# Gate and up by Strassen's seven products of 256 columns, second product in chunks of eight feature blocks

## The chip, the cores and the metric

The kernel runs on one core of one Trainium2 chip. The metric is the device time of one execution in microseconds. A core has five engines with instruction streams of their own: PE (TensorE, matrix products; its weight loads are listed apart as PEld), DVE (VectorE), ACT (ScalarE), POOL (GpSimd) and SP (SyncE, here only a queue that issues DMA transfers). Each engine works through its stream in order; semaphores join the streams.

## The reference, cut to what matters

512 tokens of width 1024 go through two layers. Per layer:

```
x <- x + 1/2 * SwiGLU_1(RMSNorm(x))
h  = RMSNorm(x);  P = h @ W_in          (gMLP, short convolution and retention mixers on P)
x <- x + concat(A, B, C) @ W_out
x <- x + 1/2 * SwiGLU_2(RMSNorm(x))
SwiGLU(x) = (silu(x @ w_gate) * (x @ w_up)) @ w_down        w_gate, w_up: 1024 x 2816, w_down: 2816 x 1024
```

A final RMSNorm follows. So there are four feed-forwards and two mixers, all in float32.

## The kernel before, in words

Activations lie with features on the 128 partitions and the 512 tokens along the free axis: x is eight tiles of 128x512 (`KT` = 8), the hidden layer 22 tiles (`FT` = 22, "feature blocks"). Every product is made of three matrix products: each operand is split into a high part in float32r (`xh`, `whi`, the left side of `h`) and the rest (`xl`, `wlo`), and `mm3` (L99 to L101) adds high*high, high*rest and rest*high into one PSUM bank. The split of an operand is a cast on ACT (L93 for weights, L113 for x) and a subtraction on DVE (L94, L114).

`gate_up` (L148) loops over the 22 feature blocks; for each it loads a gate and an up block of 128x1024 weights (512 KB each, `load`, four raw buffers, three pairs of split ones), does 24 matmuls of 512 columns for each, and `finish` scales by the token's 1/rms (`rr`), applies silu, multiplies and splits the result into `h`. When all 22 `h` exist, `ffn` (L216) runs the second product: eight output blocks `d`, each 66 matmuls of 512 columns, and after each the residual add and, in `after(d)`, the split of the new `x[d]` for the next stage and its square. 1/rms is made of those squares while the next stage's first blocks are multiplied: `norm_columns` (`pss`, L130) and `norm_rows` (`psr`, L144) each add a few small matmuls. `last_ffn` runs the last second product with tokens on partitions, in all eight PSUM banks. `start` (L187) lets the first products begin on half a weight block and the first x tile.

The order in which each engine issues is made by a scheduler when the program is built: it takes instructions by their place in the code and moves loads and splits ahead as far as buffers and its own estimate of times let it. Buffers are handed out by tag, a fixed number each.

Of the kernel before, what the change touches and what calls it, by code (L numbers as in the profile page):

```python
# [36 lines left out]
# Columns of the packed position constants.  # L37
# [5 lines left out]
def trunk(ctx, tc, xt, w_gu1, w_dn1, w_in, w_out, w_gu2, w_dn2, w_last, par, con, wst, bst, gain, out):  # L43
# [12 lines left out]
    def big(name, dt=F32):  # L56
        return hpool.tile([P, 2 * T], dt, tag="h", name=name)
# [20 lines left out]
    ct = cpool.tile([P, NCON], F32, name="ct")  # L78
# [3 lines left out]
    def weight_tiles():  # L82
        raw = wpool.tile([P, 1024], F32, tag="raw", name=uniq("raw"), bufs=4)
        hi = wpool.tile([P, 1024], F32R, tag="whi", name=uniq("whi"))
        lo = wpool.tile([P, 1024], F32R, tag="wlo", name=uniq("wlo"))
        return raw, hi, lo

    def load(src):
        """One block of weights as two float32r parts whose sum it is."""
        n = src.shape[-1]  # L90
        raw, hi, lo = weight_tiles()
        nc.sync.dma_start(raw[:, :n], src)
        nc.scalar.copy(hi[:, :n], raw[:, :n])  # L93
        nc.vector.tensor_tensor(lo[:, :n], raw[:, :n], hi.bitcast(F32)[:, :n], ALU.subtract)  # L94
        return hi, lo
# [7 lines left out]
    def split(h, lo, src):  # L103
        nc.scalar.copy(h, src)  # L104
        nc.vector.tensor_tensor(lo, src, h.bitcast(F32), ALU.subtract)  # L105
# [4 lines left out]
    def norm_part(k, gcol):  # L110
        """x[k] times its gain in two parts."""
        g = pcol[:, gcol + k : gcol + k + 1]
        nc.scalar.activation(xh[k], x[k], AF.Copy, scale=g)  # L113
        nc.vector.scalar_tensor_tensor(xl[k], x[k], g, xh[k].bitcast(F32), ALU.mult, ALU.subtract)  # L114

    def squares(k):
        if k == 0:
            state["acc"] = spool.tile([P, T], F32, tag="acc", name=uniq("acc"), bufs=1)
            nc.scalar.activation(state["acc"], x[k], AF.Square)
        else:  # L120
            sq = tpool.tile([P, T], F32, tag="sq", name=uniq("sq"))
            nc.scalar.activation(sq, x[k], AF.Square)
            nc.vector.tensor_tensor(state["acc"], state["acc"], sq, ALU.add)

    def norm_columns():
        """1 / rms of each token, as columns [token, chunk]."""
# [22 lines left out]
    def gate_up(l, w_gu, first=False):  # L149
        """h = silu(rms gate) * up, features on partitions."""  # L150
        hs = []
        waiting = []

        def finish(ps):
            rr = state["rr"]
            a = tpool.tile([P, T], F32, tag="a", name=uniq("a"))
            nc.vector.tensor_tensor(a, ps[0], rr, ALU.mult)  # L157
            nc.scalar.activation(a, a, AF.Silu)  # L158
            b = tpool.tile([P, T], F32, tag="b", name=uniq("b"))
            nc.vector.tensor_tensor(b, ps[1], a, ALU.mult)  # L160
            h = big(uniq("h"), F32R)
            split(h[:, :T], h[:, T:], b)
            hs.append(h)

        for f in range(FT):
            ps = []
            if first and f == 0:
                ps = start(w_gu[l, 0, 0], w_gu[l, 1, 0])
            else:
                for j in range(2):  # L170
                    hi, lo = load(w_gu[l, j, f])
                    p = bank(uniq("pgu"))
                    for k in range(KT):
                        c = slice(k * P, (k + 1) * P)
                        mm3(p, hi[:, c], lo[:, c], xh[k], xl[k], k == 0, k == KT - 1)
                    ps.append(p)
                    if f == 0 or first and f == 1:
                        (norm_columns, norm_rows)[j]()
            waiting.append(ps)
            if "rr" in state:  # L180
                while waiting:
                    finish(waiting.pop(0))
            yield hs

    def start(gate, up):
# [16 lines left out]
        for k in range(4, KT):
            nc.sync.dma_start(x[k], xt[:, k, :])
        for k in range(KT):
            norm_part(k, G1)
            for (raw, hi, lo), p in zip(w, ps):
                if k % 4 == 0:
                    c = half[k // 4]
# [4 lines left out]
        for k in range(KT):  # L213
            squares(k)
# [389 lines left out]
```

## Time and profile before

| | |
|---|---|
| median of 3 runs | 1877.07 us (1877.07 to 1877.4) |
| span of the profiled execution | 1875.7 us |
| PE, weight loads | 1865.6 us busy (99%), 1554.4 us (83%) |
| DVE, ACT, POOL | 839.3 us (45%), 567.2 us (30%), 27.4 us (1%) |
| DMA | 181.98 MB, 97 GB/s mean |

The profiled execution's own time is taken as its span, first to last instruction; the runs' median lies 1.4 us above it. Matmuls are pipelined, so a busy PE need not be at its peak: the spacing of matmul starts tells more than the busy share.

### The profile page before, as it was taken

To read this page: it belongs to the slowest core of one execution; us is meant where nothing else is said; L and a number is where in the kernel's file an instruction comes from. 1 tells how busy PE (TensorE), PEld (TensorE's weight loads), DVE (VectorE), ACT (ScalarE), POOL (GpSimd) and SP (SyncE) were. 2 spreads that over 40 slices of the span, in tenths; PEclk is the share of its full clock that TensorE was granted. 3 is DMA by queue.
4 is the path that set the end of the run, shared out by engine and by line. 5 is a ranking of instruction groups with operands and counts; after the bars stand their busy time and mean duration, and the time that the engine had idled before them with its cause. 6 is when DMAs were issued, how large, how long until landed. Compare 5 with 4: busy or idle time off the path is not lost.

```text
span 1875.7 us, 20497 instructions
## 1 busy us (share of the span) xinstructions
PE 1865.6 (99%) x8560; PEld 1554.4 (83%) x8560; DVE 839.3 (45%) x1052; ACT 567.2 (30%) x713; POOL 27.4 (1%) x34
## 2 busy tenths in 40 slices
PE   9999999999999999999999999999999999999998
PEld 7888888888888888888888888888888888888886
DVE  5344334474664434433443444344647543444224
ACT  5223222223343322322232232222132433323212
POOL 0000000000000000000000000000000000000000
PEclk9999999999999999999999999999999999999999
DMA  5232333322222232233323223333322222332321
GB/s 203 102 97 94 99 93 93 114 94 75 84 90 97 95 101 91 99 93 95 106 90 102 91 100 96 94 93 108 102 79 79 91 92 89 100 100 92 113 94 64
DMA packets 52860, 181.98 MB, mean 97 GB/s; under 512 B 6048, under 2 KB 6560, under 8 KB 52640
## 3 DMA queue, kind: packets, MB, share of 16 engines
q1 hardware_dynamic: 52624, 180.64, 29.8%
q8 instruction: 67, 1.10, 0.2%
q14 instruction: 25, 0.20, 0.0%
q10 hardware_dynamic: 144, 0.04, 0.0%
HBM read 178.56 MB, written 2.10 MB: 96 GB/s over the span
## 4 chain that ended last, share of the span: by engine, by line
PE 98%; issue 0%; ACT 0%; DMA 0%; DVE 0%; SPq 0%; POOL 0%; POOLq 0%; ACTq 0%
PE pgu L99 17%; PE pgu L100 17%; PE pgu L101 17%; PE pdn L101 8%; PE pdn L100 8%; PE pdn L99 8%; PE pqk L99 2%; PE pqk L101 2%; PE pout L100 2%; PE pout L99 2%; PE pqk L100 2%; PE pout L101 2%; PE pv L101 1%; PE pg L99 1%; PE pg L101 1%; PE pg L100 1%
## 5 line engine op out<-in xcount | busy, mean ns | idle before, releaser
L93 ACT CAST whi<-raw 128x1024 fp32r<-128x1024 f32 (+1 forms) x336 | 348.6, 1038 | 1184.7 <-issue 365.1
L99 PE MATMUL pgu<-xh,whi 128*128 128x512 f32 x1408 | 548.6, 390 | 1.2 <-ACT xh L113 1.2
L100 PE MATMUL pgu<-xl,whi 128*128 128x512 f32 x1408 | 548.0, 389 | 0.7 <-DVE xl L114 0.6
L94 DVE TENSOR_TENSOR wlo<-raw,whi 128x1024 fp32r<-128x1024 f32 (+1 forms) x336 | 405.1, 1206 | 319.3 <-ACT whi L93 305.2
L101 PE MATMUL pgu<-xh,wlo 128*128 128x512 f32 x1408 | 548.0, 389 | 0.0
L99 PEld LDWEIGHTS pgu<-xh,whi 128*128 128x128 f32 x1408 | 264.2, 188 | 56.4 <-ACT xh L113 1.7
L100 PEld LDWEIGHTS pgu<-xl,whi 128*128 128x128 f32 x1408 | 264.3, 188 | 55.8 <-DVE xl L114 1.5
L101 PEld LDWEIGHTS pgu<-xh,wlo 128*128 128x128 f32 x1408 | 264.3, 188 | 55.5 <-DVE wlo L210 0.3
L99 PE MATMUL pdn<-h,whi 128*128 128x512 f32 x528 | 205.4, 389 | 0.0
L100 PE MATMUL pdn<-h,whi 128*128 128x512 f32 x528 | 205.4, 389 | 0.0
L101 PE MATMUL pdn<-h,wlo 128*128 128x512 f32 x528 | 205.4, 389 | 0.0
L160 DVE TENSOR_TENSOR b<-pgu,a 128x512 f32<-128x512 f32 x88 | 60.8, 692 | 280.2 <-PE pgu L101 277.8
L157 DVE TENSOR_TENSOR a<-pgu,rr 128x512 f32<-128x512 f32 x88 | 60.8, 691 | 220.0 <-PE pgu L101 220.0
L100 PEld LDWEIGHTS pdn<-h,whi 128*128 128x128 f32 x528 | 99.1, 188 | 20.6
L101 PEld LDWEIGHTS pdn<-h,wlo 128*128 128x128 f32 x528 | 99.1, 188 | 20.6
L99 PEld LDWEIGHTS pdn<-h,whi 128*128 128x128 f32 x528 | 99.1, 188 | 20.5
L100 PE MATMUL pdn<-wlo,h 128*128 128x512 f32 x176 | 68.6, 390 | 0.0
L101 PE MATMUL pdn<-whi,h 128*128 128x512 f32 x176 | 68.5, 389 | 0.0
L99 PE MATMUL pdn<-whi,h 128*128 128x512 f32 x176 | 68.4, 389 | 0.0
L105 DVE TENSOR_TENSOR h<-b,h 128x512 fp32r<-128x512 f32 x88 | 60.2, 685 | 2.1 <-ACT h L104 2.1
L104 ACT CAST h<-b 128x512 fp32r<-128x512 f32 x88 | 54.7, 622 | 2.7 <-DVE b L160 2.5
L158 ACT ACTIVATE a<-a 128x512 f32<-128x512 f32 x88 | 55.0, 626 | 1.3 <-DVE a L157 1.3
(179 smaller groups left out, 1641.9 us busy)
## 6 DMA issues: line engine op xcount, KB each, us to landing
raw<-in_w_gu SPq DMA_DIRECT2D x174, 512.0 KB, 3.3
raw<-in_w_in SPq DMA_DIRECT2D x52, 512.0 KB, 3.3
raw<-in_w_dn SPq DMA_DIRECT2D x48, 448.0 KB, 3.3
raw<-in_w_dn SPq DMA_DIRECT2D x24, 512.0 KB, 3.5
raw<-in_w_last SPq DMA_DIRECT2D x22, 512.0 KB, 3.3
raw<-in_w_out SPq DMA_DIRECT2D x16, 512.0 KB, 3.3
x<-in_xt SPq DMA_DIRECT2D x8, 256.0 KB, 6.6
out<-o SPq DMA_DIRECT2D x8, 256.0 KB, 2.2
```

Of the source, the lines that this page charges most:

```text
L93: nc.scalar.copy(hi[:, :n], raw[:, :n])
L94: nc.vector.tensor_tensor(lo[:, :n], raw[:, :n], hi.bitcast(F32)[:, :n], ALU.subtract)
L99: nc.tensor.matmul(ps, lhsT=ah, rhs=bh, start=first, stop=False)
L100: nc.tensor.matmul(ps, lhsT=ah, rhs=bl, start=False, stop=False)
L101: nc.tensor.matmul(ps, lhsT=al, rhs=bh, start=False, stop=last)
L104: nc.scalar.copy(h, src)
L105: nc.vector.tensor_tensor(lo, src, h.bitcast(F32), ALU.subtract)
L157: nc.vector.tensor_tensor(a, ps[0], rr, ALU.mult)
L158: nc.scalar.activation(a, a, AF.Silu)
L160: nc.vector.tensor_tensor(b, ps[1], a, ALU.mult)
```

## The change

x, a 1024 x 512 matrix, and each pair of 1024 x 256 weight blocks are cut in halves along features and along tokens, so that a gate (or up) result of 256 features x 512 tokens is a 2 by 2 block product. Instead of its eight block products of 256 columns (24 matmuls each with the three parts, in the kernel before as 2 x 24 of 512 columns) it is made of seven (Strassen's, in Winograd's form): 7 x 4 pairs of x tiles x 3 parts = 84 matmuls of 256 columns. The unit is called a quad here; there are 22 per feed-forward (11 pairs of feature blocks, gate and up), 88 in all.

- x needs sums of its quarters: `norm_pair` makes, for each pair of x tiles, the forms S1, S2, S3, Z4 in float32 on DVE (128x256 each) and splits them; only ahead of a feed-forward (`sums`).
- The weights need sums: `load_quad` loads four quarters of 128x512 (columns A to D), loads the last one twice more, has a DMA from POOL add B and C to those copies, makes two more sums on DVE, and splits seven operands: `wd` and `wp` of 128x1024, `we`, `wf`, `wg` of 128x512.
- The results are put together from PSUM: products 1, 6, 7 and 4 add up in bank `pa`, 2 in `pb`, 5 and 3 in `pc`, and after each one ACT or DVE copies, adds or subtracts a quarter of 128x256 (L256 to L268). `WHEN` sets the order: product 1, 2 of a quad, 3 of the quad before, 6, 5, 4 of the quad before, 7. The tables `MOVING` and `WHEN` name them by number.
- The second product runs in three chunks of 8, 8 and 6 feature blocks after the gate and up of each, and adds to x three times; squares and norms follow the last chunk, once per pair of x tiles. Buffers: two raw weight tiles of 128x2560, three split tiles `w2`, five `w1`; work tiles come from pools opened per stage. `start` no longer starts on halves. In the mixer, the constants are loaded in each layer and the scores are made earlier.

```
-PIECES = ((0, 8), (8, 15), (15, 22))
+CHUNKS = ((0, 4), (4, 8), (8, 11))
+A11, A21, A12, A22, S1, S2, S3, Z4 = range(8)
...
+    def load_quad(src):
+        c = KP * P
+        raw = wpool.tile([P, 2560], F32, tag="raw", name=uniq("rawq"), bufs=2)
+        s = [raw[:, i * c : (i + 1) * c] for i in range(5)]
+        nc.sync.dma_start(raw[:, : 3 * c], src[:, : 3 * c])
+        two = raw[:, 3 * c :].rearrange("p (n c) -> p n c", n=2)
+        nc.sync.dma_start(two, src[:, 3 * c :].unsqueeze(1).broadcast_to([P, 2, c]))
+        nc.gpsimd.dma_start(raw[:, 3 * c :], src[:, c : 3 * c], accum_op=ALU.add)
+        d = wpool.tile([P, 2048], F32R, tag="w2", name=uniq("wd"), bufs=3)
+        parts(d[:, :1024], d[:, 1024:], raw[:, : 2 * c])
+        e = wpool.tile([P, 1024], F32R, tag="w1", name=uniq("we"), bufs=5)
+        parts(e[:, :c], e[:, c:], s[2])
+        nc.vector.tensor_tensor(s[2], s[2], s[3], ALU.add)
+        f = wpool.tile([P, 1024], F32R, tag="w1", name=uniq("wf"), bufs=5)
+        parts(f[:, :c], f[:, c:], s[2])
+        p = wpool.tile([P, 2048], F32R, tag="w2", name=uniq("wp"), bufs=3)
+        parts(p[:, :1024], p[:, 1024:], raw[:, 3 * c :])
+        nc.vector.tensor_tensor(s[0], s[0], s[2], ALU.add)
+        g = wpool.tile([P, 1024], F32R, tag="w1", name=uniq("wg"), bufs=5)
+        parts(g[:, :c], g[:, c:], s[0])
...
+    def norm_pair(m, gcol, sums):
+        xf[m] = xpool.tile([P, 16 * H], F32R, tag=f"xf{m}", name=uniq("xf"))
+        for k in (2 * m, 2 * m + 1):
+            g = pcol[:, gcol + k : gcol + k + 1]
+            nc.scalar.activation(xh(k), x[k], AF.Copy, scale=g)
+            nc.vector.scalar_tensor_tensor(xl(k), x[k], g, xh(k).bitcast(F32), ALU.mult, ALU.subtract)
+        if not sums:
+            return
+        v = spool.tile([P, 4 * T], F32, tag="xv", name=uniq("xv"), bufs=1)
+        for k in (0, 1):
+            g = pcol[:, gcol + 2 * m + k : gcol + 2 * m + k + 1]
+            nc.scalar.activation(v[:, k * T : (k + 1) * T], x[2 * m + k], AF.Copy, scale=g)
+        q = [v[:, i * H : (i + 1) * H] for i in range(8)]
+        nc.vector.tensor_tensor(q[S1], q[A21], q[A22], ALU.subtract)
+        nc.vector.tensor_tensor(q[S2], q[S1], q[A11], ALU.subtract)
+        nc.vector.tensor_tensor(q[S3], q[A11], q[A21], ALU.subtract)
+        nc.vector.tensor_tensor(q[Z4], q[S2], q[A12], ALU.add)
+        parts(xf[m][:, 4 * H : 8 * H], xf[m][:, 12 * H :], v[:, 2 * T :])
...
+    MOVING = {1: A11, 2: A12, 3: Z4, 4: A22, 5: S1, 6: S2, 7: S3}
+    WHEN = {1: 0, 2: 1, 6: 3, 5: 4, 7: 6, 3: 9, 4: 12}
+
+    def product(ps, n, w, first, pairs=range(KP)):
+        hi, lo = w[n]
+        for m in pairs:
+            bh, bl = form(m, MOVING[n])
+            c = slice(m * P, (m + 1) * P)
+            one = first and m == pairs[0]
+            nc.tensor.matmul(ps, lhsT=hi[:, c], rhs=bh, start=one, stop=False, skip_group_check=True)
+            nc.tensor.matmul(ps, lhsT=hi[:, c], rhs=bl, start=False, stop=False, skip_group_check=True)
+            nc.tensor.matmul(ps, lhsT=lo[:, c], rhs=bh, start=False, stop=m == pairs[-1], skip_group_check=True)
...
+            if n == 1:
+                nc.scalar.copy(c(A11), b["pa"])
+            elif n == 2:
+                nc.vector.tensor_tensor(c(A11), b["pb"], c(A11), ALU.add)
+            elif n == 6:
+                nc.scalar.copy(c(A12), b["pa"])
+            elif n == 5:
+                nc.scalar.copy(c(A22), b["pc"])
+            elif n == 7:
+                nc.vector.tensor_tensor(c(A22), c(A22), b["pa"], ALU.subtract)
+            elif n == 3:
+                nc.vector.tensor_tensor(c(A12), b["pc"], c(A12), ALU.subtract)
             else:
...
+                nc.scalar.copy(c(A21), b["pa"])
+                done(q)
...
+    def ffn(l, w_gu, w_dn, after):
+        with tc.tile_pool(name=uniq("ffn"), bufs=1, reuse_waits="tile") as pool:
+            stage["pool"] = pool
+            for i, (p0, p1) in enumerate(CHUNKS):
+                hs = gate_up(w_gu[l], p0, p1, i == 0)
+                down(l, w_dn, 2 * p0, hs, after if p1 == FP else lambda d: None)
```

`done` does what `finish` did, on 128x1024: for a gate quad the product with `rr` (L276, DVE) and silu (L277, ACT), for an up quad the product with the gate (L280, DVE) and the split into `h`.

DVE within gate and up. Before, the order repeats after two weight blocks (`wlo` a weight's rest, `a`, `b`, `h` the block's silu, product and split):

```order
L94 TENSOR_TENSOR wlo_794<-raw_792,whi_793 128x1024
L160 TENSOR_TENSOR b_756<-pgu_728,a_753 128x512
L94 TENSOR_TENSOR wlo_833<-raw_831,whi_832 128x1024
L105 TENSOR_TENSOR h_758<-b_756,h_758 128x512
L157 TENSOR_TENSOR a_823<-pgu_767,rr_323 128x512
L94 TENSOR_TENSOR wlo_864<-raw_862,whi_863 128x1024
```

In the change, one quad's share of the same stage; `g_`, `u_` are results of gate and up quads, `raw..885` the weights of the next quad but one to be multiplied:

```order
L88 TENSOR_TENSOR wd_889<-rawq_885,wd_889 128x1024
L88 TENSOR_TENSOR h_750<-u_528,h_750 128x1024
L258 TENSOR_TENSOR u_766<-pb_802,u_766 128x256
L88 TENSOR_TENSOR wp_899<-rawq_885,wp_899 128x1024
L266 TENSOR_TENSOR g_646<-pc_722,g_646 128x256
L88 TENSOR_TENSOR we_892<-rawq_885,we_892 128x512
L114 TENSOR_TENSOR rawq_885<-rawq_885 128x512
L119 TENSOR_TENSOR rawq_885<-rawq_885 128x512
L88 TENSOR_TENSOR wf_896<-rawq_885,wf_896 128x512
L276 TENSOR_TENSOR g_646<-g_646,rr_324 128x1024
L264 TENSOR_TENSOR u_766<-u_766,pa_788 128x256
L88 TENSOR_TENSOR wg_903<-rawq_885,wg_903 128x512
```

Two weight subtractions of 128x1024 per two blocks became two of 128x1024 and three of 128x512, two sums (L114, L119) and three steps from PSUM (L258, L266, L264) came in between, and `wp`, `L114` and what follows them wait for the adding DMA.

ACT in the same place. Before, a cast of weights alternates with a silu or a split of `h`:

```order
L93 CAST whi_622<-raw_621 128x1024
L104 CAST h_548<-b_546 128x512
L93 CAST whi_653<-raw_652 128x1024
L158 ACTIVATE a_613<-a_613 128x512
L93 CAST whi_692<-raw_691 128x1024
```

In the change, one quad's share; L256, L260, L262 and L268 are the copies out of PSUM:

```order
L87 CAST wg_785<-rawq_767 128x512
L87 CAST wd_889<-rawq_885 128x1024
L87 CAST h_750<-u_528 128x1024
L256 COPY u_766<-pa_788 128x256
L87 CAST wp_899<-rawq_885 128x1024
L87 CAST we_892<-rawq_885 128x512
L260 COPY u_766<-pa_788 128x256
L87 CAST wf_896<-rawq_885 128x512
L262 COPY u_766<-pc_842 128x256
L268 COPY g_646<-pa_668 128x256
```

The copy of product 1 (L256), which frees `pa` for product 6, now stands behind the casts of `wg` and `wd` and the split of `h` (or the silu).

DVE at the start of the program. Before, the splits of x (L114), the first half weights (L210) and the squares (L123) follow each other:

```order
L114 SCALAR_TENSOR_TENSOR xl_94<-x_78,pcol,xh_86 128x512
L114 SCALAR_TENSOR_TENSOR xl_95<-x_79,pcol,xh_87 128x512
L123 TENSOR_TENSOR acc_219<-acc_219,sq_224 128x512
L210 TENSOR_TENSOR wlo_132<-raw_130,whi_131 128x512
L210 TENSOR_TENSOR wlo_135<-raw_133,whi_134 128x512
L123 TENSOR_TENSOR acc_219<-acc_219,sq_227 128x512
L114 SCALAR_TENSOR_TENSOR xl_96<-x_80,pcol,xh_88 128x512
L114 SCALAR_TENSOR_TENSOR xl_97<-x_81,pcol,xh_89 128x512
```

In the change, 12 of the 48 DVE instructions that stand ahead of the first step out of PSUM; `xf` and `xv` are the forms of x and their sums for pair 0 (101), 1 (120, 125), 2 (139, 144) and 3 (158, 163):

```order
L88 TENSOR_TENSOR xf_139<-xv_144,xf_139 128x1024
L88 TENSOR_TENSOR wf_191<-rawq_180,wf_191 128x512
L119 TENSOR_TENSOR rawq_180<-rawq_180 128x512
L170 TENSOR_TENSOR xv_163<-xv_163 128x256
L168 TENSOR_TENSOR xv_163<-xv_163 128x256
L88 TENSOR_TENSOR wd_206<-rawq_202,wd_206 128x1024
L169 TENSOR_TENSOR xv_163<-xv_163 128x256
L88 TENSOR_TENSOR wg_198<-rawq_180,wg_198 128x512
L171 TENSOR_TENSOR xv_163<-xv_163 128x256
L88 TENSOR_TENSOR we_209<-rawq_202,we_209 128x512
L88 TENSOR_TENSOR wp_216<-rawq_202,wp_216 128x1024
L88 TENSOR_TENSOR xf_158<-xv_163,xf_158 128x1024
```

The splits of the first two quads' weights stand between the sums of the x pairs, and the split of pair 3's sums (`xf_158`) comes last.

## Rows read from the trace of the kernel before

**Rows 1.** The page: span, busy time by engine, granted clock by slice, chain by engine.
```profile
span 1875.7 us, 20497 instructions
...
PE 1865.6 (99%) x8560; PEld 1554.4 (83%) x8560; DVE 839.3 (45%) x1052; ACT 567.2 (30%) x713; POOL 27.4 (1%) x34
...
PEclk9999999999999999999999999999999999999999
...
PE 98%; issue 0%; ACT 0%; DMA 0%; DVE 0%; SPq 0%; POOL 0%; POOLq 0%; ACTq 0%
```

**Rows 2.** Chain that ended last, in order of time: start us, us, what.
```profile
25.76 0.79 PE pss L130 x8
...
375.80 0.79 PE pss L130 x8
...
581.64 0.79 PE pss L130 x8
...
942.57 0.79 PE pss L130 x8
...
1303.48 0.79 PE pss L130 x8
...
1860.47 0.76 DVE xtok L277
```

**Rows 3.** Timeline of PE in gate and up, 512 columns, first and last of 37 matmuls: start us, us, what.
```profile
17.21 0.39 PE L101 MATMUL pgu<-xh,wlo 128*128 128x512 f32 x1
...
25.37 0.39 PE L101 MATMUL pgu<-xh,wlo 128*128 128x512 f32 x1
```

**Rows 4.** Timeline of PE at the gMLP values, 256 columns, first and last of 64 matmuls.
```profile
441.66 0.28 PE L100 MATMUL pav<-wlo,xh 128*128 128x256 f32 x1
...
449.22 0.28 PE L100 MATMUL pav<-wlo,xh 128*128 128x256 f32 x1
```

**Rows 5.** Windows: us, busy of PE, PEld, DVE, ACT, POOL, clock, DMA share, GB/s.
```profile
400.00:430.00 30.00, 30.00 (x134) 24.86 (x133) 17.51 (x22) 5.58 (x6) 0.00 (x0) 1.00 0.30 97
...
438.60:450.10 11.50, 11.50 (x99) 11.50 (x97) 2.50 (x5) 4.34 (x6) 0.00 (x0) 1.00 0.14 47
...
589.50:820.00 230.50, 230.50 (x1018) 190.85 (x1017) 95.59 (x109) 69.41 (x88) 0.00 (x0) 1.00 0.29 95
```

**Rows 6.** Groups by shape on DVE and ACT: busy us, mean ns, idle before.
```profile
L94 DVE TENSOR_TENSOR wlo<-raw,whi 128x1024 fp32r<-128x1024 f32 x288 | 352.7, 1225 | 244.6 <-ACT whi L93 233.0
...
L93 ACT CAST whi<-raw 128x1024 fp32r<-128x1024 f32 x288 | 303.2, 1053 | 1003.6 <-issue 365.1 <-PE pgu L100 333.0 <-PE pdn L101 82.8
...
L114 DVE SCALAR_TENSOR_TENSOR xl<-x,pcol,xh 128x512 fp32r<-128x512 f32 x48 | 35.6, 750 | 22.5 <-ACT xh L113 22.5
...
L113 ACT ACTIVATE xh<-x,pcol 128x512 fp32r<-128x512 f32 x48 | 34.3, 721 | 42.2 <-DVE x L230 38.8 <-DMA x<-in_xt 1.8 <-DMA pcol<-in_par 1.7
...
L123 DVE TENSOR_TENSOR acc<-acc,sq 128x512 f32<-128x512 f32 x42 | 29.0, 691 | 0.2
...
L386 ACT ACTIVATE av<-pav,rc 128x256 f32<-128x256 f32 x8 | 3.8, 475 | 12.9 <-PE pav L101 12.9
...
L357 DVE TENSOR_TENSOR qx<-q,ct 128x384 f32<-128x384 f32 x8 | 3.9, 552 | 0.0
...
L143 DVE TENSOR_SCALAR dg<-ident,rc 128x128 f32<-128x128 f32 x24 | 5.3, 282 | 6.9 <-POOL rc L134 6.9
...
L505 ACT ACTIVATE lsq<-av 128x1024 f32<-128x1024 f32 x2 | 2.1, 1061 | 13.3 <-DVE av L503 13.3
...
L210 DVE TENSOR_TENSOR wlo<-raw,whi 128x512 fp32r<-128x512 f32 x4 | 2.6, 687 | 0.3 <-ACT whi L209 0.3
...
L209 ACT CAST whi<-raw 128x512 fp32r<-128x512 f32 x4 | 2.3, 610 | 0.0
```

**Rows 7.** Chain piece of the start, and two windows there.
```profile
2.19 6.27 DMA x<-in_xt
...
6.00:10.00 4.00, 2.74 (x11) 1.34 (x9) 2.06 (x4) 2.17 (x5) 0.00 (x0) 1.00 0.97 333
...
10.00:15.00 5.00, 4.39 (x18) 3.22 (x18) 5.00 (x9) 5.00 (x10) 0.00 (x0) 1.00 1.03 388
```

**Rows 8.** DMA issues of gate and up weights: KB each, us from issue to landing.
```profile
raw<-in_w_gu SPq DMA_DIRECT2D x174, 512.0 KB, 3.3
```

**Rows 9.** Timeline of DVE at the norm of the second feed-forward.
```profile
582.47 0.16 DVE L132 TENSOR_SCALAR ms<-pss 128x4 f32<-128x4 f32 x1 [2.87 <-PE pss L130]
...
583.75 0.88 DVE L143 TENSOR_SCALAR dg<-ident,rc 128x128 f32<-128x128 f32 x4 [1.12 <-POOL rc L134]
```

More of the change, by code (lines that the diff above doesn't have):

```diff
@@ L101, in mm3 @@
         nc.tensor.matmul(ps, lhsT=al, rhs=bh, start=False, stop=last)
[L103 to L105 removed]
+    split = parts
     state = {}
     warm_ps = bank("warm")
[L110 to L114, printed above, removed]
@@ L123, in squares @@
-            nc.vector.tensor_tensor(state["acc"], state["acc"], sq, ALU.add)
+            for i in range(2):
+                nc.vector.tensor_tensor(state["acc"], state["acc"], sq[:, i * T : (i + 1) * T], ALU.add)
     def norm_columns():
@@ L147, in norm_rows @@
         state["rr"] = rr
[L149 to L168, printed above, removed]
-            else:
[L170 to L183, printed above, removed]
@@ new lines, in down @@
+    def down(l, w_dn, f0, hs, after):
+        rr = state["rr"]
+        n = len(hs)
+        pieces = [(i, min(i + 8, n)) for i in range(0, n, 8)]
+        for d in range(KT):
+            p = bank(uniq("pdn"))
+            for a, b in pieces:
+                hi, lo = load(w_dn[l, d, :, (f0 + a) * P : (f0 + b) * P])
+                for f in range(a, b):
+                    c = slice((f - a) * P, (f - a + 1) * P)
+                    mm3(p, hi[:, c], lo[:, c], hs[f][0], hs[f][1], f == 0, f == n - 1)
+            y = spool.tile([P, T], F32, tag="y", name=uniq("y"))
+            nc.vector.scalar_tensor_tensor(y, p, 0.5, rr, ALU.mult, ALU.mult)
+            nc.vector.tensor_tensor(x[d], x[d], y, ALU.add)
+            after(d)
@@ L204, in start @@
[L204 to L208, printed above, removed]
-                    nc.scalar.copy(hi[:, c], raw[:, c])
-                    nc.vector.tensor_tensor(lo[:, c], raw[:, c], hi.bitcast(F32)[:, c], ALU.subtract)
-                c = slice(k * P, (k + 1) * P)
-                mm3(p, hi[:, c], lo[:, c], xh[k], xl[k], k == 0, k == KT - 1)
-        for k in range(KT):
-            squares(k)
@@ L215, in start @@
-        return ps
-    def ffn(l, w_gu, w_dn, after, first=False):
-        state.pop("rr", None)
-        *_, hs = gate_up(l, w_gu, first)
-        rr = state["rr"]
-        for d in range(KT):
-            p = bank(uniq("pdn"))
-            for f0, f1 in PIECES:
-                hi, lo = load(w_dn[l, d, :, f0 * P : f1 * P])
-                for f in range(f0, f1):
-                    c = slice((f - f0) * P, (f - f0 + 1) * P)
-                    mm3(p, hi[:, c], lo[:, c], hs[f][:, :T], hs[f][:, T:], f == 0, f == FT - 1)
-            y = tpool.tile([P, T], F32, tag="b", name=uniq("y"))
-            nc.vector.scalar_tensor_tensor(y, p, 0.5, rr, ALU.mult, ALU.mult)
-            nc.vector.tensor_tensor(x[d], x[d], y, ALU.add)
-            after(d)
+        for m in range(KP):
+            nc.sync.dma_start(xp[m], xt[:, 2 * m : 2 * m + 2, :])
+            norm_pair(m, G1, True)
+            squares(m)
@@ L256, in last_ffn, with part @@
[L256 to L258 removed]
+        def part(ps, w, h, n, s, first, last):
             hi, lo = w
             t, c = slice(n * P, (n + 1) * P), slice(s * T, (s + 1) * T)
[L261 to L268 removed]
@@ L353, in mixer @@
             nc.scalar.activation(tok(vt, n), p, AF.Copy, scale=rc[:, n : n + 1])
-        qx = [big(uniq("qx")) for _ in range(2)]
+        sc = [big(uniq("sc")) for _ in range(2)]
+        for n in range(NCH):
+            p = bank(uniq("psc"))
+            t = slice(n * P, (n + 1) * P)
+            for h in range(HEADS):
+                nc.tensor.matmul(p[:, h * P : (h + 1) * P], lhsT=head(1, h)[:, t], rhs=head(0, h)[:, t], start=True, stop=True)
+            nc.vector.tensor_tensor(tok(sc, n), p, ct[:, C_DEC : C_DEC + T], ALU.mult)
+        qx = qk[:2]
         for h in range(HEADS):
```

313 lines of the change are left out of this document (195 added, 118 removed).

## The prediction, on record before the run

> **What bounds the kernel now.** I read the page first. PE is busy for 99% of the span, the chain by engine is PE for 98%, and the granted clock is at its upper level in every slice [rows 1]. Nothing on DVE, ACT or DMA ends a wait that matters. The chain in order of time then gives the length of a whole feed-forward: from 942.57 to 1303.48 it takes 360.9 us [rows 2], in which PE runs 1056 matmuls for gate and up and 528 for the second product. The timeline of PE gives their spacing: 36 spacings from 17.21 to 25.37 are 0.2267 us each [rows 3]. 1584 x 0.2267 = 359.1, and the other 1.8 us are the norm's small matmuls. So inside a feed-forward there is no stall to win; what counts is how many matmuls there are and how far apart they start.
>
> **What seven products save.** The nearest row for a float32r matmul of 256 columns is the gMLP value product: 63 spacings from 441.66 to 449.22, 0.1200 us each [rows 4]. That is more than half of 0.2267 (0.1133). The windows show why: with 512 columns the weight loads are busy for 24.86 of 30 us, with 256 for 11.50 of 11.50 [rows 5], so the load and no longer the columns sets the pace. Two feature blocks of gate (or up) cost 48 x 0.2267 = 10.88 us before, a quad costs 84 x 0.1200 = 10.08. The change takes away an eighth of the columns but 7% of the time: 0.80 us x 88 quads = 70.4 us. Bounds: at 0.1133 it would be 9.52 and 120 us, at 0.1295 nothing. I take 0.1200, since operands, types and the three parts are the same there.
>
> The Trainium skill, TensorE: Matmul & The Clock Gate, section Back-to-back issue gap, has 262 cycles for 256 columns and 518 for 512 when warm, 109 and 216 ns. By it the saving would be 88 x (48 x 0.216 - 84 x 0.109) = 106 us. This trace has 120 and 227 ns, and the measurement decides.
>
> **What it adds per quad, and what hides it.** On DVE, by the groups [rows 6]: two subtractions of 128x1024 at 1.225, three of 128x512 at 0.687, two sums of 128x512 at 0.691, together 5.89 us. The three steps of 128x256 out of PSUM have no row; 128 columns take 0.282 and 384 take 0.552, so I take 0.42 each, 1.26. The gate quad then has 1.225 more, the up quad 2.45: 8.4 and 9.6 us, 9.0 in the mean. On ACT: two casts at 1.053 and three at 0.610, four copies out of PSUM at most 0.475 each, one pass of 128x1024 at 1.06: 6.9 us. Both fit under 10.08 us of PE. Before, DVE had 95.59 of 230.5 us there [rows 5], 4.5 us per two blocks. DVE goes from 41% to about 90%, so it is nearly a second bound; were the PSUM steps 0.55 as in the wider row, 9.4.
>
> Order matters as well as sums. ACT's copy of product 1 stands behind the casts of `wg` and `wd` and the silu or split. `wd` may start when product 7 of the quad before has ended: 0.3 + 1.05 + 1.06 + 0.48 puts the copy's end near 2.9 us of a quad's time, and product 6, which needs the bank, starts after three products, 4.3 us. Cover 1.4 us. The split of `wd` is needed a whole quad later. Steady state costs nothing by this.
>
> **What it adds at the edges.**
>
> Start of the program. Each pair of x tiles now takes DVE 2 x 0.75 + 4 x 0.42 + 1.225 + 2 x 0.69 = 5.8 us [rows 6], four pairs 22.5 (the first adds one square less), and nine weight steps and sums stand between them in the order shown (two `wd`, two `wp`, four of 512 and two sums, 9.0 us). That is 31.5 us of DVE before pair 3's forms are split. DMA is no limit: 10:15 moves 388 GB/s [rows 7], so 2 MB of x and two quads' weights are there by about 16 us. DVE starts near 6 us, and the single `xv` buffer makes ACT and DVE take turns, so I put the last form at 38 us. Until then PE can do 66 matmuls (products 1 and 2 of two quads, 5 and 6 of the first without pair 3), 7.9 us: 30 us are lost. Before, PE reached `pss` at 25.76 [rows 2] with 72 matmuls of 0.2267 done: 9.4 lost. The difference is 20.6, with the wait for `psr` 22. Between 18 (DVE instructions that overlap by some 8%) and 30 (the first 66 matmuls at the lower clock level, which no window here shows).
>
> Second feed-forwards, twice. After the last output product DVE still has, in its order, the add, `wg`, `wd`, one split of x, four sums, two squares, `we`, one PSUM step, L114, `wp`, and pair 3's subtraction: about 10.5 us. PE has 66 matmuls and `pss`, 8.7 us. Then `psr` needs the chain of `ms`, POOL and `dg`, 2.2 us [rows 9], behind other DVE work. 4 us each, 8 in all (0 to 7 each).
>
> First feed-forward of layer 2. Its x pairs come out of a six-block chunk: PE needs 36 x 0.2267 = 8.16 us per pair, DVE 5.8 + 4 x 0.69 + 2 x 0.95 (weights of 768 columns) = 10.5. Three pairs fall behind by 2.3 each, and then comes the start as above: 10 us (4 to 16).
>
> Chunk ends. The last pair's `h` takes a copy, a product, a cast and a subtraction, 0.48 + 1.225 + 1.05 + 1.225 = 4.0 us. In an eight-block chunk 18 matmuls (4.1 us) are ready meanwhile, in a six-block one only 12 (2.7): 1.3 x 3, and 0.3 for each of the other nine, 7 us. Residual adds go from 8 to 24 per feed-forward, beside PE. Mixers: the same matmuls, fewer work buffers, 1 us each. The tail after the last matmul keeps its steps.
>
> Sum: -70.4 + 22 + 8 + 10 + 7 + 2 = -21.4 on a span of 1875.7, so 1854.3; the median of the runs lies 1.4 above the span: **1856 us**, 1.1% faster.
>
> **The rivals.**
>
> 1. The adding DMA is slow and the quads wait for weights (slower). Two raw buffers mean that one buffer must go round in two quads, 20.2 us: loads of 1.3 MB (3.4 us at the rate of [rows 7] plus about 2), the add, then 7 us of splits and sums up to `wg`. That leaves 7.8 us for the add. No such DMA is in this trace; a plain load of the same 512 KB takes 3.3 us [rows 8], and if the add reads its target as well and takes twice that, 6.6, it just fits. Beyond 7.8 each microsecond costs half a microsecond per quad, 44 us; the gain is gone at 8.3. At 9 us: 1856 + 53 = 1909. For it: DVE's and ACT's queues stand behind `wp`, so every delay reaches all later steps. Against it: DMA is busy for 0.29 of the time in this stage [rows 5]. Chance 0.18.
>
> The Trainium skill, SBUF — State Buffer, section Who interferes with whom, says that DMAs issued from POOL starve while DVE runs copies or `tensor_scalar` in a two-port mode, but not during `tensor_tensor`. DVE's rows in the changed quads are all `tensor_tensor`; no run so far shows either.
>
> 2. The edges cost half as much again (start 33, the others 38 together): 71 us, as much as is saved, 1877. For it: four norms on a DVE that is full. Against it: the order keeps matmuls of earlier pairs ready. Chance 0.13, about half of it within 0.2%.
>
> 3. The weight load does not set the pace here, because two of three matmuls use the same weights, and 256 columns take half of 512: 49 us more are saved, 1807. Against it: the load count equals the matmul count in this kernel [rows 1], though there too two of three share weights. Chance 0.05.
>
> **How the numbers follow.** The forecast has 0.64; with its bounds (start 18 to 30, others 4 to 40) it reaches from 1838 to 1880. The range 1836 to 1900 leaves out rival 3 and the upper half of rival 1. A change of 0.2%, 3.8 us, is about what a measurement of this kernel can tell from none. Faster: 0.64 less 0.02 for its own upper end, rival 3 and a quarter of rival 2, 0.70; same: half of rival 2 and a little of the others, 0.08; slower: 0.22.
>
> **What would show it.** In the changed trace: spacing of the gate and up matmuls 0.120; quads 10.1 us apart with no wait of PE on DVE, ACT or DMA in between; first `pss` near 35 us or later, with DVE full from 6 us on; after each norm a PE wait of 3 to 10 us, the longest at the first feed-forward of layer 2; a DVE share of about 70%; the add landing within 7 us of its issue. Wrong would make it: a period over 10.3 us in the middle of a chunk, whatever ends the wait, or a spacing other than 0.120.

## Result, and the profile after

The changed kernel takes 1942.43 us (median of 4 runs) against 1877.22 for the kernel before beside it: a ratio of 1.0348, 95% interval 1.0328 to 1.0369, 3.5% slower. The forecast of 1856 us had the wrong sign. Two of its four runs took 1938.6 us, the profiled one among them (span 1936.5), and two 1946 to 1947, so differences against the median of 1942 are good to some 4 us.

The page of the changed kernel: span, busy time, granted clock by slice, POOL's DMA queue (packets, MB, share of 16 engines' span), chain by engine. It answers to [rows 1].

```profile
span 1936.5 us, 28563 instructions
...
PE 1836.3 (95%) x11728; PEld 1677.9 (87%) x11728; DVE 1294.2 (67%) x1813; ACT 836.9 (43%) x1263; POOL 105.2 (5%) x122
...
PEclk7999999999999999999999999999999999999999
...
q0 software_dynamic: 12672, 46.14, 14.1%
...
PE 73%; DMA 11%; DVE 9%; issue 3%; ACT 3%; POOL 1%; SPq 0%; POOLq 0%; DVEq 0%; ACTq 0%
```

PE is no longer busy throughout (99% before), and DMA, which had 0% of the chain before, has 11%. DVE is at 67%, as forecast (about 70%), so its average load does not explain the loss.

Who waited for whom, PE and then one group of ACT: engine, tile and line, what it waited for: us in all, times, longest.

```profile
PE pa L219 <- ACT u L260: 32.2, 9, 5.7
PE pa L297 <- ACT wd L87: 26.7, 4, 11.6
PE psv L589 <- POOL ws L581: 11.6, 2, 5.8
...
ACT wp L87 <- DMA rawq<-in_w_gu: 74.1, 11, 9.5
```

`pa L219 <- ACT u L260` is product 7 of an up quad, which adds onto product 6 in bank `pa` and so must wait until ACT has copied that out (L260). `pa L297` is the first product of a feed-forward; its longest wait, 11.6 us, is the start of the program. `psv` belongs to the mixers. ACT itself waited 74.1 us in 11 places for a DMA before the cast of `wp`, the two operands that hold the adding DMA's sums.

To see how much each place costs I took the spacing of every two matmul starts beyond the undisturbed 0.2267 us (512 columns), 0.1200 (256) or 0.1116 (128), and added it up by stage (a gap between two stages counts with one of the two). All in us; the last three columns are experiments below.

```
                                        before   after  DVE sums  + early ws  + first pair plain
first matmul on weights starts at          6.2    18.2      18.1        18.2         8.9
first gate/up chunk, feed-forward 1        3.2    11.8       9.3         9.3        10.2
  the same, 2 / 3 / 4                 0.1 each  9.3/14.1/8.2  1.4/10.4/1.4  1.4/10.3/1.4  1.4/1.0/1.4
the other eight gate/up chunks               -    56.1      -0.1        -0.1        -0.1
second products                            0.1     5.1       1.5         1.5         1.5
two mixers                                -1.5    16.5      17.5         1.1         1.1
sum without the first line                 1.9   121.2      41.3        24.7        16.5
  of it at the lower clock level           0      24.0       7.4         5.7         4.3
```

The sum closes: 1875.7 - 70.4 (the saving as forecast) + 12.0 (first matmul later) + 119.3 (121.2 - 1.9) = 1936.6, and the span is 1936.5. So the saving is there in full, and what ate it are stalls: 90 us in gaps of over 0.25 us, and 24 us of slow matmuls behind them.

The largest item, 56.1, is for the most part one and the same gap early in each chunk that does not open a stage. The second chunk of the first feed-forward shows it. Timelines of SP, POOL, ACT, DVE and PE there: start us, us, engine, what, and in brackets the idle time before it and what ended it.

```profile
161.23 0.33 SPq L106 DMA_DIRECT2D rawq<-in_w_gu  x1
161.61 0.43 SPq L108 DMA_DIRECT2D rawq<-in_w_gu  x1
167.10 0.33 SPq L106 DMA_DIRECT2D rawq<-in_w_gu  x1
167.47 0.94 SPq L108 DMA_DIRECT2D rawq<-in_w_gu  x1
...
167.47 0.86 POOL L109 DMA_DIRECT2D rawq<-in_w_gu  x1 [13.33 <-DVE g L264]
...
167.45 0.38 ACT L256 COPY u<-pa 128x256 f32<-128x256 f32 x1 [0.34 <-PE pa L221]
175.98 1.04 ACT L87 CAST wp<-rawq 128x1024 fp32r<-128x1024 f32 x1 [8.16 <-DMA rawq<-in_w_gu]
...
177.45 0.36 ACT L260 COPY u<-pa 128x256 f32<-128x256 f32 x1
...
168.96 0.42 DVE L258 TENSOR_TENSOR u<-pb,u 128x256 f32<-128x256 f32 x1 [0.42 <-PE pb L221]
177.06 1.23 DVE L88 TENSOR_TENSOR wp<-rawq,wp 128x1024 fp32r<-128x1024 f32 x1 [7.67 <-ACT wp L87]
...
170.13 0.28 PE L219 MATMUL pa<-xf,wf 128*128 128x256 f32 x1
...
174.33 0.28 PE L221 MATMUL pa<-xf,wg 128*128 128x256 f32 x1
177.87 0.58 PE L219 MATMUL pa<-xf,wp 128*128 128x256 f32 x1 [3.26 <-ACT u L260]
178.25 0.42 PE L220 MATMUL pa<-xf,wp 128*128 128x256 f32 x1
178.46 0.41 PE L221 MATMUL pa<-xf,wp 128*128 128x256 f32 x1
...
180.60 0.37 PE L219 MATMUL pa<-xf,wd 128*128 128x256 f32 x1
...
190.75 0.28 PE L219 MATMUL pa<-xf,wd 128*128 128x256 f32 x1
...
200.83 0.28 PE L219 MATMUL pa<-xf,wd 128*128 128x256 f32 x1
...
210.91 0.28 PE L219 MATMUL pa<-xf,wd 128*128 128x256 f32 x1
```

The third quad's loads leave at 161.23, since only then one of two raw buffers is free (L106 brings columns A to C, 768 KB, L108 two copies of D, 512 KB). Its adding DMA (L109) needs both loads and leaves at 167.47 (the bracket names a DVE step that ended just then), beside the fourth quad's loads, issued at 167.10 and 167.47. It has landed when ACT, idle for 8.16 us, is let go on to cast `wp`, 8.5 us after its issue, and only behind that cast in ACT's order stands the copy L260, which PE has needed since 174.6. From 170.13 to 174.33 lie 35 spacings of 0.1200, the forecast spacing; behind the gap they are 0.21. The last four rows are the first matmuls of quads (`wd`): 10.15, 10.08 and 10.08 us apart, the period that the prediction had for the middle of a chunk.

Why the buffer came free so late stands in four earlier rows of POOL and DVE:

```profile
143.31 0.86 POOL L109 DMA_DIRECT2D rawq<-in_w_gu  x1 [52.65 <-DVE we L88]
153.28 0.86 POOL L109 DMA_DIRECT2D rawq<-in_w_gu  x1 [9.11 <-DVE rawq L114]
...
158.78 0.69 DVE L114 TENSOR_TENSOR rawq<-rawq 128x512 f32<-128x512 f32 x1 [2.46 <-issue]
159.99 1.22 DVE L88 TENSOR_TENSOR wp<-rawq,wp 128x1024 fp32r<-128x1024 f32 x1
```

The first quad's add was issued at 143.31, beside the second quad's loads, and landed at 152.29, 9.0 us later; the second quad's add left only at 153.28 and landed at 158.70. DVE, which works in order, stood until then before the second quad's sum (L114) and split `wp` of the first quad, the last reader of that quad's buffer, only behind it. So the third quad's loads left 5.2 us after the chunk's first matmul (156.04): the adds of the first two quads had used up the lead.

The windows around that gap (us; busy of PE, PEld, DVE, ACT, POOL; granted clock; DMA share; GB/s):

```profile
160.00:174.00 14.00, 12.61 (x105) 12.61 (x106) 8.89 (x13) 4.98 (x9) 0.86 (x1) 1.00 0.71 191
...
177.90:180.50 2.60, 2.60 (x12) 2.60 (x13) 2.53 (x5) 0.53 (x1) 0.05 (x1) 0.50 0.76 110
181.00:240.00 59.00, 57.95 (x481) 57.54 (x480) 46.49 (x65) 31.75 (x56) 3.46 (x4) 1.00 0.56 150
```

The clock of the matmuls behind the gap is at its lower level, 1.2 GHz (0.50), for 2.6 us in this window, and at the upper one from 181 on. The same loop of two raw buffers that fails at the chunk's start keeps up in its middle, but for one wait of 1.2 us near the end of the chunk (from 229.51).

### The profile page after: what moved, and what is told of

It is laid out like the page before. It is cut to its first block, busy times and chain, and to the rows that moved or that the text cites. A ratio compares the mean times of both kernels' runs of the same rounds, so it can differ in the third digit from the quotient of the medians.

```text
span 1936.5 us, 28563 instructions
## 1 busy us (share of the span) xinstructions
PE 1836.3 (95%) x11728; PEld 1677.9 (87%) x11728; DVE 1294.2 (67%) x1813; ACT 836.9 (43%) x1263; POOL 105.2 (5%) x122
## 3 DMA queue, kind: packets, MB, share of 16 engines
q0 software_dynamic: 12672, 46.14, 14.1%
## 4 chain that ended last, share of the span: by engine, by line
PE 73%; DMA 11%; DVE 9%; issue 3%; ACT 3%; POOL 1%; SPq 0%; POOLq 0%; DVEq 0%; ACTq 0%
DMA rawq<-in_w_gu 10%; PE pa L219 8%; PE pa L221 7%; PE pa L220 7%; PE pdn L135 6%; PE pdn L134 6%; PE pdn L136 6%; PE pc L219 4%; PE pc L221 4%; PE pc L220 4%; PE pb L219 2%; PE pb L220 2%; PE pb L221 2%; PE pqk L134 2%; PE pqk L136 2%
## 5 line engine op out<-in xcount | busy, mean ns | idle before, releaser
L87 ACT CAST w<-raw 128x1024 fp32r<-128x1024 f32 (+1 forms) x162 | 165.4, 1021 | 445.4 <-PE pdn L136 195.8
L88 DVE TENSOR_TENSOR w<-raw,w 128x1024 fp32r<-128x1024 f32 (+1 forms) x162 | 191.6, 1182 | 137.7 <-ACT w L87 137.1
L135 PE MATMUL pdn<-h,w 128*128 128x512 f32 x528 | 205.7, 391 | 0.0
L134 PE MATMUL pdn<-h,w 128*128 128x512 f32 x528 | 205.7, 391 | 0.0
L136 PE MATMUL pdn<-h,w 128*128 128x512 f32 x528 | 205.3, 390 | 0.0
L88 DVE TENSOR_TENSOR wp<-rawq,wp 128x1024 fp32r<-128x1024 f32 x88 | 107.7, 1224 | 131.8 <-ACT wp L87 131.7
L87 ACT CAST wp<-rawq 128x1024 fp32r<-128x1024 f32 x88 | 92.2, 1048 | 182.9 <-DMA rawq<-in_w_gu 74.1
L109 POOL DMA_DIRECT2D rawq<-in_w_gu x88 | 76.7, 872 | 1376.1 <-DVE we L88 451.3
L219 PE MATMUL pa<-xf,wp 128*128 128x256 f32 x352 | 105.9, 301 | 35.6 <-ACT u L260 32.2
L135 PEld LDWEIGHTS pdn<-h,w 128*128 128x128 f32 x528 | 99.2, 188 | 21.6 <-DVE h L88 1.7
L134 PEld LDWEIGHTS pdn<-h,w 128*128 128x128 f32 x528 | 99.2, 188 | 20.9 <-ACT h L87 0.8
L136 PEld LDWEIGHTS pdn<-h,w 128*128 128x128 f32 x528 | 99.2, 188 | 20.4
L114 DVE TENSOR_TENSOR rawq<-rawq 128x512 f32<-128x512 f32 x88 | 60.8, 691 | 78.3 <-DMA rawq<-in_w_gu 65.3
L87 ACT CAST wd<-rawq 128x1024 fp32r<-128x1024 f32 x88 | 92.6, 1052 | 46.1 <-PE pdn L136 27.0
L88 DVE TENSOR_TENSOR wd<-rawq,wd 128x1024 fp32r<-128x1024 f32 x88 | 107.5, 1221 | 2.2 <-ACT wd L87 2.1
L219 PE MATMUL pa<-xf,wf 128*128 128x256 f32 x352 | 100.9, 287 | 4.9 <-ACT g L256 4.8
L219 PEld LDWEIGHTS pa<-xf,wp 128*128 128x128 f32 x352 | 70.9, 202 | 39.2 <-ACT u L260 34.0
L221 PE MATMUL pa<-xf,wp 128*128 128x256 f32 x352 | 103.5, 294 | 0.0
L220 PE MATMUL pa<-xf,wp 128*128 128x256 f32 x352 | 103.4, 294 | 0.0
L221 PE MATMUL pc<-xf,wp 128*128 128x256 f32 x352 | 100.0, 284 | 1.7 <-DVE wp L88 1.7
```

The lines of the kernel that those rows point to most:

```text
L87: nc.scalar.copy(hi, src)
L88: nc.vector.tensor_tensor(lo, src, hi.bitcast(F32), ALU.subtract)
L109: nc.gpsimd.dma_start(raw[:, 3 * c :], src[:, c : 3 * c], accum_op=ALU.add)
L114: nc.vector.tensor_tensor(s[2], s[2], s[3], ALU.add)
L219: nc.tensor.matmul(ps, lhsT=hi[:, c], rhs=bh, start=one, stop=False, skip_group_check=True)
L220: nc.tensor.matmul(ps, lhsT=hi[:, c], rhs=bl, start=False, stop=False, skip_group_check=True)
```

## Experiments

Each is timed against the kernel before on the same chip (median 1877.02 to 1877.21).

**No addition at all.** The adding DMA is left out and nothing put in its place.

```
-        nc.gpsimd.dma_start(raw[:, 3 * c :], src[:, c : 3 * c], accum_op=ALU.add)
```

> Leaves out the adding DMA and puts nothing in its place, so that the operands of four of the seven products lack a summand; every other instruction stays. Theory A: what the adding DMA costs in all, 1865 to 1885, a little below the run with DVE sums. Theory B: DVE and ACT have the same work as before, 1942.

1855.99 us, ratio 0.9887 (0.9872 to 0.9902). The stalls sum to 36.9, with none left in the eight later chunks. Theory B falls: DVE and ACT do the same work as in the changed kernel, and 86 us are gone.

**The sums on DVE.**

```
-        nc.gpsimd.dma_start(raw[:, 3 * c :], src[:, c : 3 * c], accum_op=ALU.add)
+        nc.vector.tensor_tensor(raw[:, 3 * c :], raw[:, 3 * c :], raw[:, c : 3 * c], ALU.add)
```

> The adding DMA of each quad is replaced by one DVE addition of 128x1024; the 768 KB and 512 KB loads, the buffers and the products stay. Theory A (the quads at the start of a chunk or stage wait for weights, because load and adding DMA, 5.7 to 9 us for the latter, come one after the other in only two raw buffers and DVE and ACT stand in order behind them): the waits on the raw buffers and about half of the 121 us of PE stalls go, 1942 becomes 1870 to 1895, although DVE gets 88 x 1.2 = 106 us more work. Theory B (DVE and ACT are simply too full, 67% and 43% on average and more in gate and up): 1942 or slower, up to 2040.

1858.07 us, ratio 0.9899 (0.9884 to 0.9913): with every sum made it is 1.0% faster than the kernel before, and faster still than theory A had it. Its page, busy time and chain:

```profile
PE 1812.5 (98%) x11728; PEld 1659.7 (89%) x11728; DVE 1390.2 (75%) x1901; ACT 857.1 (46%) x1263; POOL 26.4 (1%) x34
...
PE 92%; DVE 5%; ACT 1%; POOL 1%; issue 1%; DMA 1%; SPq 0%; POOLq 0%; ACTq 0%
```

A window in its second chunk (columns as above):

```profile
150.00:230.00 80.00, 80.00 (x655) 79.42 (x654) 68.92 (x92) 44.11 (x73) 0.00 (x0) 1.00 0.37 119
```

DVE has 96 us more work than in the changed kernel. In the middle of gate and up it is busy for 68.92 of 80 us, 86%, and PE waits for nothing.

**A plain transfer in its place.** The third transfer copies, so that two sums are left out.

```
-        nc.gpsimd.dma_start(raw[:, 3 * c :], src[:, c : 3 * c], accum_op=ALU.add)
+        nc.gpsimd.dma_start(raw[:, 3 * c :], src[:, c : 3 * c])
```

> The third transfer of each quad stays on POOL's queue, behind the same two loads, with the same 512 KB, but it copies and does not add (so two sums are left out). Theory A1 (adding makes the transfer slow): its landing falls from 5.7 us towards 3.5 and most of the 84 us come back, 1865 to 1885. Theory A2 (what costs is a third transfer that may only be issued when two others have landed, whatever it does): 1915 to 1942.

1881.15 us, ratio 1.0025 (1.0016 to 1.0035). Of the 84 us between the changed kernel and the one with DVE sums, 61 go with the adding, and 23 with the third transfer as such (25 against the run with no third step at all). The page of this kernel, POOL's queue (packets, MB, share of 16 engines' span):

```profile
q0 software_dynamic: 12672, 46.14, 7.5%
```

Its DMA issues (KB each, median us to landing):

```profile
rawq<-in_w_gu POOLq DMA_DIRECT2D x88, 512.0 KB, 4.0
```

And those of the changed kernel:

```profile
rawq<-in_w_gu SPq DMA_DIRECT2D x88, 768.0 KB, 4.7
rawq<-in_w_gu SPq DMA_DIRECT2D x88, 512.0 KB, 6.1
rawq<-in_w_gu POOLq DMA_DIRECT2D x88, 512.0 KB, 5.7
```

The same 46.14 MB occupied the 16 engines for 7.5% of 1879.7, 141 us, as a copy, and for 14.1% of 1936.5, 273 us, as an addition: 1.9 times as long. To landing it is 4.0 against 5.7 us in the median. How the 23 us divide between the third transfer's own time and its wait for the other two was not tried.

**DVE sums only in the first two quads of each chunk.** 24 of 88 quads take the DVE line, 64 the adding DMA.

```
+        if early:
+            nc.vector.tensor_tensor(raw[:, 3 * c :], raw[:, 3 * c :], raw[:, c : 3 * c], ALU.add)
+        else:
+            nc.gpsimd.dma_start(raw[:, 3 * c :], src[:, c : 3 * c], accum_op=ALU.add)
...
-            live[q] = {"w": load_quad(w_gu[p, j]), "c": c}
+            live[q] = {"w": load_quad(w_gu[p, j], q < 2), "c": c}
```

> The first two quads of each of the 12 chunks make the two weight sums on DVE (24 of 88 quads); the other 64 keep the adding DMA. If the adding DMA costs only where no weights lie ahead, at the start of a chunk: 1856 to 1868. If it costs in the middle of a chunk as well: in proportion, 64 of 88 parts of 84 us stay, 1910 to 1925.

1879.36 us, ratio 1.0014 (1.0005 to 1.0024): 63 of 84 us come back with 27% of the quads. That is neither figure. By stage (not in the table), six of the eight later chunks have no gap left and two have one, in the last feed-forward (5.0 and 4.5); the first chunks of feed-forwards 1 and 3 have 14.3 and 15.8 against 9.3 and 10.4 with DVE sums everywhere. So adding DMAs from the third quad on cost nothing in six chunks. What differs there is when the third quad's loads can leave. SP and PE in the second chunk of this run, its first matmul last:

```profile
156.51 0.33 SPq L106 DMA_DIRECT2D rawq<-in_w_gu  x1
...
158.69 0.28 PE L222 MATMUL pa<-xf,wd 128*128 128x256 f32 x1
```

They leave 2.2 us before that matmul (1.4 to 2.2 in the six chunks), where in the changed kernel they leave 5.2 us after it (1.9 to 5.6 in all eight); and the third add of this chunk lands 5.6 us after its issue, not 8.4. In the last feed-forward of this run they leave 2.1 us after it, and the gap is there. Why they are late there even with DVE sums, and what the add adds to the sums of x in the first chunks, was not taken apart.

**The gMLP weights.** Load (L574 to L579) and masking (L581) go ahead of the first convolution.

```
+        wsm = big(uniq("ws"))
+        nc.sync.dma_start(ws, wst[l])
...
         def conv(j):
...
         conv(0)
-        wsm = big(uniq("ws"))
-        nc.sync.dma_start(ws, wst[l])
...
```

> Only the load of the gMLP's token weights and their masking on POOL move, in each mixer, from behind the first convolution to ahead of it. Theory: each mixer's 5.96 us stall between pbg and psv and the lower clock level behind it go, 2 x (6 + 1): 1928 to 1930. Rival: the wait only moves to the convolution's own loads, which share the queue: 1942.

1925.85 us, ratio 1.0255 (1.024 to 1.027): 16.6 us less by the medians and 12.2 by the profiled spans (1936.5 and 1924.3), and the mixers' stalls go from 16.5 to 1.1. That is the theory, with a mixer's stall a little dearer than its 7 us. The run with DVE sums, which has the first of these two stalls at 501.38 as the changed kernel has it at 518.88, shows in the timelines of SP, POOL and PE what was late:

```profile
497.04 5.44 SPq L94 DMA_DIRECT2D raw<-in_w_in  x2
502.53 0.42 SPq L574 DMA_DIRECT2D ws<-in_wst  x1
...
506.68 1.56 POOL L581 TENSOR_SCALAR_AFFINE_SELECT ws<-ws 128x128 f32<-128x128 f32 x4 [8.46 <-DMA ws<-in_wst]
...
501.38 0.39 PE L136 MATMUL pbg<-xf,w 128*128 128x512 f32 x1
507.56 2.73 PE L589 MATMUL psv<-ws,av 128*64 128x128 f32 x18 [5.79 <-POOL ws L581]
```

Behind two loads of the convolution's weights, which hold SP from 497.04 to 502.48, the gMLP weights' transfer is issued only at 502.53, more than a microsecond after PE's last `pbg` matmul has started; POOL masks them from 506.68 on, and PE's next product starts at 507.56.

**Chunks without Strassen.** No sums of x or weights; everything but gate and up as in the changed kernel.

```
+                for i in range(2):
+                    hi, lo = load(w_gu[p, j][:, i * 2 * T : (i + 1) * 2 * T])
+                    ps = bank(uniq("pgu"))
+                    for k in range(KT):
+                        o = (1 - k % 2) * T + k // 2 * P
+                        mm3(ps, hi[:, o : o + P], lo[:, o : o + P], xh(k), xl(k), k == 0, k == KT - 1)
```

> Chunks of 8, 8 and 6 feature blocks, two raw buffers, mixer and start as in the changed kernel, but gate and up by eight products of 512 columns, with no sums of x or of weights. Theory A: the restructuring alone costs little, 1880 to 1900. Theory C (chunks and fewer buffers stall PE whatever the product): the 121 us of stalls stay in good part, 1930 to 1980.

1905.03 us, ratio 1.015 (1.0133 to 1.0167). The stalls are the two mixers (17.0 of 22.1) and a first matmul at 13.7 instead of 6.2. Gate and up and the second products in chunks cost 2.6 + 2.5, so theory C falls. What lies above the expectation are the mixers' 17 us, which it did not have.

**Both mended**: the edits of the runs with DVE sums and early gMLP weights together.

> Sums of weights on DVE in all quads, and the gMLP weights loaded ahead of the first convolution. If the two costs are separate: 1858 - 14 = 1843 to 1845.

1841.94 us, ratio 0.9813 (0.9798 to 0.9828). The costs are separate. What is left are the start and the first feed-forward of layer 2 (table). Windows of this kernel there:

```profile
6.00:18.00 12.00, 0.23 (x3) 0.04 (x1) 11.84 (x22) 12.00 (x17) 0.00 (x0) 0.63 0.73 283
18.00:28.00 10.00, 5.13 (x21) 4.79 (x22) 10.00 (x15) 6.50 (x10) 0.00 (x0) 0.50 0.00 0
911.00:931.00 20.00, 13.45 (x61) 11.11 (x60) 20.00 (x35) 14.90 (x20) 0.00 (x0) 0.91 0.39 133
```

DVE is busy for 11.84 of 12, 10.00 of 10 and 20.00 of 20 us while PE waits. In the first window ACT is full as well (12.00 of 12), and it is ACT's cast of `wd` that the first matmul waits for; in the other two ACT has room, and DVE is the bound.

**Sums behind the first products.** In the code of `gate_up`, behind products 1 and 2 of the first two quads (`later` holds the splits of a quad other than `wd`); at the program's start the squares also come behind the splits of all x, in this run and in the next:

```
+            later[0]()
+            if gsum is not None:
+                for m in range(KP):
+                    make_sums(m, gsum)
+            later[1]()
...
-            norms = [norm_columns, norm_rows]
+            norms = [lambda: None] * 3 + [norm_columns, norm_rows]
```

> As the run with DVE sums and early gMLP weights, and in both first feed-forwards the sums of x and the other five weight operands of the first two quads come behind the splits of x and of wd; the norm's products come three products later; at the program's start the first quads' loads stand between those of x. If the start and the first feed-forward of layer 2 lose their time because ACT and DVE make sums ahead of what the first products need: 12 to 20 us less, 1823 to 1832. Rival: the work is only put off and products 5 and 6 wait for it: 1838 to 1848.

1851.71 us, ratio 0.9866 (0.9851 to 0.9881): the rival. The first matmul starts at 8.9 instead of 18.2, but the first chunk then has 25.3 us of stalls instead of 9.3, and feed-forward 3 14.3 instead of 10.3. The work was only put off.

**The first pair of feature blocks without Strassen**, in the first feed-forward of each layer:

```
+        if gsum is not None:
+            finish = plain(w_gu[p0], gsum, hs)
+            p0, fresh = p0 + 1, False
```

`plain` makes gate and up of two blocks by `mm3` over k (the first two blocks side by side), with the calls that make the sums of x between the first two blocks and the others.

> As the run with DVE sums and early gMLP weights, but in the first feed-forward of each layer the first pair of feature blocks (two of 22 quads) is made by eight products of 512 columns, which need no sums of x or of weights; the sums of x are made beside them, and at the start two blocks' loads stand between those of x. Theory (the start and the first feed-forward of layer 2 lose 21 and 10 us because DVE must make sums before PE can go on): the start comes to 10 or 12 us, the other to 1 or 2, four quads cost 0.8 us more each: 1842 - 10 - 8.5 + 3.2 = 1822 to 1832. Rival: DVE has no room for the sums beside the plain products either and products 5 and 6 of the next quads wait: 1836 to 1846.

1827.1 us, ratio 0.9731 (0.9715 to 0.9747), 2.7% faster than the kernel before and the best of all. Its page:

```profile
PE 1808.9 (99%) x11584; PEld 1648.3 (90%) x11584; DVE 1370.6 (75%) x1865; ACT 849.5 (47%) x1243; POOL 26.4 (1%) x34
...
PE 97%; DVE 1%; ACT 1%; issue 1%; POOL 0%; DMA 0%; POOLq 0%; ACTq 0%; DVEq 0%
```

Two of its windows, at the start and at the first feed-forward of layer 2:

```profile
6.00:18.00 12.00, 9.09 (x26) 6.74 (x27) 11.25 (x16) 11.64 (x16) 0.00 (x0) 0.72 0.74 264
916.00:936.00 20.00, 20.00 (x90) 16.56 (x89) 18.49 (x29) 14.22 (x19) 0.00 (x0) 1.00 0.43 136
```

Here PE has 9.09 of 12 us at the start where it had 0.23 in the run with both mended, and 20.00 of 20 at the first feed-forward of layer 2 where it had 13.45, with DVE nearly as full: four quads that need no sums give DVE the time to make them.

## Why the prediction was wrong

**The step that failed** is the price of the adding DMA: "Two raw buffers mean that one buffer must go round in two quads, 20.2 us", from which the sum put its cost at nothing and rival 1 at half a microsecond per quad beyond 7.8 us. Measured, it costs 84 us (1942 to 1858 without it), 61 of them for the adding. The loop was rightly set up, and even its condition was met: the add lands 5.7 us after its issue in the median, and in the middle of a chunk the quads run nearly without a wait. What the step left out is that the loop is entered twelve times. While the second product runs, both raw buffers are in its service; two quads can be fetched ahead, but their adds run beside each other's loads (9.0 us for the first) and hold both buffers past the chunk's first matmul. The third quad's load, add and cast then follow each other with nothing in reserve, and its add shares the DMA engines with the next loads and takes 8.5 us. That the loss sits at the chunk starts and comes from the adding was shown (two runs that take it away; one that takes it away in the first two quads). That the gap reaches PE by way of ACT's order, the copy L260 behind the cast of `wp`, is read from the timeline and was not tried by itself, nor was a third raw buffer. Rival 1 named the right transfer, with 0.18, but not the place, and priced it at 1909: it counted steady quads, and not the clock, which stood at its lower level behind most of the gaps; the matmuls at that level took 24 us more in all. The prediction's own signs of being wrong, a period over 10.3 us in the middle of a chunk or another spacing, did not come: they watched the middle, and the loss was at the starts.

**Terms that held.** The saving: spacing 0.1200, and the sum above closes with 70.4. The start, in size: 12.0 + 8.6 = 20.6 in the changed kernel (11.8 less 3.2 of before) and 18.0 with DVE sums, forecast 22; the last form of x is split at 35.9, forecast 38, with DVE full as foreseen. In its order it came otherwise: ACT was full too, the first products ran at the lower clock level (0.50 in the window from 18 to 28 above), which the forecast had only in its upper bound, and `pss` comes at 27.59 after 28 matmuls and not after 35 with 66: the squares were added by 21.1. The first feed-forward of layer 2: 10.4 with DVE sums and 14.1 with the adding DMA, forecast 10 (4 to 16).

**Terms that were mis-sized.** Mixers: 1 us each, measured 9 each (16.5 + 1.5 over two). The prediction costed them as "the same matmuls, fewer work buffers" and did not follow the transfer that had been moved behind others on SP's queue. Second feed-forwards: 4 each, measured 9.3 and 8.2, and 1.4 each with DVE sums. Chunk ends: 7, measured nothing: the `h` of the last pair is ready in time. The steady DVE load: about 90% forecast, 79% measured in the changed kernel (46.49 of 59 us in the window from 181); that is why 86% was enough with the weight sums on DVE as well.

With DVE sums the forecast of 1856 would have met the 1858 measured, but that would have been luck in part: these last errors (about +16 for the mixers and -12 for second feed-forwards and chunk ends) cancel. One sum of the prediction is wrong as it stands: the bounds that it names (start 18 to 30, others 4 to 40) reach from 1829 to 1877, not from 1838 to 1880; the measured time lies beyond either.

**Rivals 2 and 3.** The edges did not cost half again by themselves. Matmuls of 256 columns stood 0.1200 apart where nothing disturbed them, so rival 3 falls. For the Trainium skill's rule that some work of DVE starves DMAs issued from POOL (SBUF — State Buffer, section Who interferes with whom) nothing speaks here: between 169.4 and 177.06 DVE did nothing at all, and the add still took 8.5 us.

## What to carry to other kernels

A loop of buffers that just closes in the steady state says nothing of its first turns: work out the third item after every change of stage, with the buffers as the first two leave them and with the transfers of its neighbours beside it. Before a slow helper takes work off an engine, look whether that engine is the bound where the work is done: an engine that was 79% busy there had room for the sums, and kept PE fed at 86%. Follow each moved transfer on its queue, small ones too. Where a cheap form needs a preparation that is not ready at a stage's start, let the plain form do the first items.

## What was unexpected of the hardware

- An adding DMA occupies the DMA engines 1.9 times as long as a plain one of the same bytes on the same queue (273 and 141 us for 46.14 MB).
- Behind a gap of 3.54 us (174.33 to 177.87) the granted clock was 0.50 and matmuls of 256 columns stood 0.21 instead of 0.12 us apart: 1.8 times, not twice. Behind the gap of 2.60 us (158.79 to 161.39) the clock stayed at 1.00 (the window from 160).
